# Spare PSUM banks behind each group of eight, later bounds for the weight splits of the attention loop, and fixed places of the y and m tiles

## The chip, the cores and the metric

The kernel runs on one core of a Trainium2 chip. The metric is the device time of one execution in microseconds (us); of several runs the median is given, with the lowest and the highest. All clock statements are about the clock granted to TensorE in the profile: 1.00 is 2.4 GHz and 0.50 is 1.2 GHz.

## The reference

Two transformer blocks run one after the other on 256 tokens of 1024 channels, in fp32. Cut to what carries the work:

```python
# block 1
h = rms_norm(x, pre_mix_norm)
mix = hybrid_mixer(h, w_in, ...)          # RG-LRU, gated linear attention, block attention
x = x + rms_norm(mix @ w_out, post_mix_norm)
h = rms_norm(x, pre_ffn_norm)
x = x + rms_norm((silu(h @ w_gate) * (h @ w_up)) @ w_down, post_ffn_norm)   # d_ff = 2816

# block 2, layers l = 0 and 1
sh1, sc1, g1, sh2, sc2, g2 = split(silu(c) @ w_ada[l] + b_ada[l], 6)
h = x * (1 + sc1) + sh1
if l == 0:
    b, cc, v = split(h @ conv_w_in, 3)
    y = (b * causal_conv3(cc * v)) @ conv_w_out
else:
    k, v, logf = shared_kv(x, c, ...)      # once
    y = forgetting_attention(h, w_q, k, v, logf, w_o)   # 16 heads, softmax(q k / 8 + F[t] - F[s]) v
x = layer_norm(alpha * x + g1 * y, ...)
h = x * (1 + sc2) + sh2
y = (silu(h @ w_gate[l]) * (h @ w_up[l])) @ w_down[l]   # d_ff = 2816
x = layer_norm(alpha * x + g2 * y, ...)
```

The three feed-forward parts are called ffn0 (block 1), ffn1 and ffn2 (block 2) below; the mixer of layer 0 is "the convolution", that of layer 1 "the attention loop".

## The kernel before

**Products.** Activations are kept transposed: a matrix of 256 tokens x 1024 channels is eight tiles of 128 channels x 256 tokens (`NK` = 8; the inner width of a feed-forward part is 22 tiles, `NFF` = 22). Each fp32 product is done in three TensorE matmuls on a split of both factors into a rounded high and a low remainder: high weights by high activation, low weights by high activation, high weights by low activation. `mm3` (L159) issues them for one weight block of 128x128 (L162, L163, L164). The activation is the moving operand, 256 columns wide.

The moving tiles have names by their role: `xh`/`xl` the input of a product, `yh`/`yl` a second set of eight (the mixer's output, or the input of a feed-forward part, by turns), `mh`/`ml` the inner activations of a feed-forward part. `hl_tiles` (L256) makes x and y tiles of T + 2 = 258 columns, of which 256 are used; the evacuation in `ffn` makes m tiles of the same size. Tiles stand in SBUF one after the other, 1056 bytes apart; the pool of the x and y tiles is `xp`, that of the m tiles the pool of each feed-forward part (`fp`).

**Weights.** There are 2336 weight blocks, in the order of use. `weights` (L130) loads them eight at a time into a raw tile (four buffers, one DMA each on SP's queue, L127), rounds them into `wh` on ScalarE (L144) and subtracts on VectorE for `wl` (L150); `wh` and `wl` have five buffers each, 4096 bytes apart in a partition.

**Vectors of the modulation.** The products with `w_ada` are matrix by vector; `gemv` (L360) does them on VectorE in 112 passes `gw` (L371), each with a load of its own on SP's queue (L368, three buffers).

**Groups.** Where the input comes tile by tile, `kouter` (L223) goes over the input tiles outside and eight output columns inside (`ksteps` L190: L197 high by high, L198 low weights, L203 or L200 low activation): eight columns of 256 fill four PSUM banks. These are all four buffers of the pool `pacc`. Every feed-forward part has such a group near its start (after a few columns done by `lazy`, L1041), the convolution one at its start. After the group the other columns of a feed-forward part come in pairs (`pair` L176: gate and up of one inner tile, 48 matmuls into one bank of `pacc`), those of the convolution as singles (`single` L168, 24 matmuls). PSUM has two more pools: `plg` with two banks (tag `lg`, the attention's logits) and `pms` with two.

**Evacuation.** `evac` in `ffn` (L906) takes gate and up out of PSUM: in ffn0 both are first multiplied by a row (L909, L911, `ff_g`, `ff_u`), then silu on ScalarE (L522), the product `ff_m` on VectorE (L914 or L918), `mh` on ScalarE (L921), `ml` on VectorE (L922). In the convolution loop (L1207 to L1224) `c_c` (L1212) and `c_up` (L1215) read PSUM.

**Attention loop** (L1304 to L1320). Each of its eight iterations i makes the next query tile (`wq`), the logits of two heads (`fox_logits` L766), the transposes of the last softmax (`fox_pt` L800, matmuls at L805), its product with the values (`fox_pv` L813), a step of the output projection, and the softmax (`fox_softmax` L784: row maxima L793, exponentials L794 on ScalarE, reciprocal L795, four scalings of `a_L` L797 on VectorE). TensorE's order is that of the code there.

**Order on the other engines.** The framework places instructions by a simulated timeline; what is fixed by hand is an order without a wait: `after(i, a)` (L383) puts i behind a on the same engine. `weights` puts each split behind an entry of the list `self.bound` once `self.free` splits have gone; `gemv` puts a pass behind `self.gbound` and behind the last split. `unbroken` (L377) sets these: ahead of the attention loop to the last gemv bound, and after its first iteration to the last row maximum of that softmax (`self.mxs`):

```python
    def unbroken(self, ins, free, act=None, head=None):
        self.bound, self.free, self.abound, self.first = ins, free, act, head
        self.gbound = ins[-1]
```

Of the kernel before, what the change touches and what calls it, by code (L numbers as in the profile page):

```python
# [9 lines left out]
F32 = mybir.dt.float32  # L10
# [4 lines left out]
ALU = mybir.AluOpType  # L15
# [20 lines left out]
EARLY = 4  # L36
EXP_LN = 6
WARM = (3, 3, 5, 0)
G_ROWS = 80
# [25 lines left out]
class Net:  # L65
# [101 lines left out]

    def single(self, wname, c, X, nk=NK, fill=True):  # L168
        t = self.acc([P, T])
        for k in range(nk):  # L170
            self.mm3(t, wname, k, c, X[0][k], X[1][k], k == 0, k == nk - 1)
        if fill:
            self.fill(nk / NK)
        return t

    def pair(self, w0, c0, w1, c1, X):  # L176
        t = self.acc([P, 2, T])
        for j, (w, c) in enumerate(((w0, c0), (w1, c1))):
            for k in range(NK):
                self.mm3(t[:, j, :], w, k, c, X[0][k], X[1][k], k == 0 and j == 0, k == NK - 1 and j == 1)  # L180
        self.fill(2)
        return t
# [49 lines left out]
    def tokmajor(self, wname, c0, nt, X):  # L232
# [21 lines left out]
        return outs  # L254

    def hl_tiles(self, tag, pool=None):  # L256

        w = T + 2
        h = self.tl(pool or self.xp, [P, w], tag + "h", F32R, NK)
        l = self.tl(pool or self.xp, [P, w], tag + "l", F32R, NK)  # L260
        return h, l, h[:, 0:T], l[:, 0:T]
# [522 lines left out]
    def fox_softmax(self, lg):  # L784

        V, A = self.nc.vector, self.nc.scalar
        mx = self.tmp("a_mx", (P, 4))
        sm = self.tmp("a_sm", (P, 4))
        Ls = [self.tmp("a_L", (P, 384), bufs=4) for _ in range(2)]
        part = [(hh, j, s) for hh in range(2) for j, s in ((0, slice(0, T)), (1, slice(T, 384)))]  # L790
        for hh, j, s in part:
            c = slice(2 * hh + j, 2 * hh + j + 1)
            self.mxs = V.tensor_reduce(mx[:, c], lg[hh][:, s], AX.X, ALU.max, negate=True)  # L793
            self.fn = A.activation(Ls[hh][:, s], lg[hh][:, s], AF.Exp, bias=mx[:, c], accum_out=sm[:, c])  # L794
        V.reciprocal(sm, sm)  # L795
        for hh, j, s in part:
            V.tensor_scalar(Ls[hh][:, s], Ls[hh][:, s], sm[:, 2 * hh + j:2 * hh + j + 1], None, ALU.mult)  # L797
        return Ls
# [101 lines left out]
    def ffn(self, l, X, R=None, first=(), rows=None):  # L900

        nc = self.nc
        V = nc.vector
        MH, ML = [], []

        def evac(g, u):  # L906
# [8 lines left out]
            else:  # L915
                s = self.silu(g)
                m = self.tmp("ff_m")
                V.tensor_tensor(m, s, u, ALU.mult)  # L918
            h = self.tl(self.fp, [P, T + 2], "mh", F32R)[:, 0:T]
            lo = self.tl(self.fp, [P, T + 2], "ml", F32R)[:, 0:T]  # L920
            nc.scalar.activation(h, m, AF.Copy)  # L921
            V.tensor_tensor(lo, m, h.bitcast(F32), ALU.subtract)  # L922
            MH.append(h)
# [11 lines left out]
        for j in range(n + 4, NFF):  # L935
            ps = self.pair(wg, j, wu, j, X)
            self.drain()
            evac(ps[:, 0, :], ps[:, 1, :])
# [140 lines left out]
    def run(self):  # L1079
# [10 lines left out]
        for k in range(NK):  # L1090
            h, l = self.hilo(self.x0[k], "x", self.vec("pre_mix_norm", k))
            X[0].append(h)
            X[1].append(l)
        for k in range(NK):
            sq = self.tmp("p_sq")
# [111 lines left out]
        for i in range(NK):  # L1207
            for w in ("ci_c", "ci_v", "ci_b"):
                if (w, i) not in got:
                    got[(w, i)] = self.single(w, i, X)  # L1210
            c = self.tmp("c_c")
# [91 lines left out]

        self.unbroken([self.gbound], 2)  # L1304
        with self.tc.manual_schedule(engines={nc.tensor.engine}):
# [3 lines left out]
            for i in range(NK + 1):  # L1309
# [7 lines left out]
                Ls = self.fox_softmax(lg) if i < NK else None  # L1317
                if i == 0:
                    self.unbroken([self.gbound, self.mxs], 0)
                q = qn  # L1320
# [164 lines left out]
```

## Time and profile before

| what | us |
|---|---|
| median of 3 runs (lowest to highest) | 987.88 (987.56 to 987.98) |
| the profiled execution, its own time | 985.9 |
| its span, first to last instruction | 984.2 |
| TensorE busy with matmuls | 927.9 (94%), 7434 matmuls |
| VectorE busy | 768.8 (78%) |
| ScalarE busy | 530.2 (54%) |
| GpSimd busy | 19.7 (2%) |
| DMA | 219.56 MB, 223 GB/s over the span |

The profile is one execution, taken by the hardware profiler. PE is TensorE (PEld its weight loads), DVE is VectorE, ACT is ScalarE, POOL is GpSimd and SP is SyncE. Times are in microseconds; a group of instructions is named by its line of the kernel, its engine, its operation and its tiles as output<-inputs. Matmuls are pipelined: one record is longer than its distance to the next, so that a pace is read from the records' number in a stretch. An entry in square brackets at the end of a timeline's row is the idle time ahead of that instruction and what ended it; "x8" merges eight instructions in a row.

### The profile page before, as it was taken

Reading aid. Unit: us, or ns where it says so; the run is one execution under the profiler, and the core shown is the slowest. Engines: PE = TensorE matmul, PEld = TensorE weight load, DVE = VectorE, ACT = ScalarE, POOL = GpSimd, SP = SyncE. Lnnn points to the kernel's source line nnn. Section 1 sums busy time; section 2 is a strip of 40 time slices with the busy share of each in tenths; the row PEclk is TensorE's granted clock in tenths of the full one; section 3 lists DMA queues with packets and bytes.
Section 4 is the critical chain, followed back from the end, with each engine's and each line's share of the span. In section 5 each row is a group of like instructions: output and inputs, shape, how many; then the busy total and the mean of one; then the engine's idle time right before and its main releaser. Section 6 shows DMA issues by size and latency. Waiting matters only on the chain.

```text
span 984.2 us, 19003 instructions
## 1 busy us (share of the span) xinstructions
PE 927.9 (94%) x7434; PEld 893.6 (91%) x7434; DVE 768.8 (78%) x1471; ACT 530.2 (54%) x951; POOL 19.7 (2%) x66
## 2 busy tenths in 40 slices
PE   7989997999999999998899999999699999999996
PEld 7879896999999899998899999987587899999995
DVE  7896678999988588679899899796764897665553
ACT  7484653554444555548555454377365586554331
POOL 1111000000000000000000000000000000000001
PEclk9999998999999999999999999999799999999998
DMA  8754337899999477544999999454642257655531
GB/s 291 249 197 129 108 108 278 294 330 327 318 336 390 142 255 250 179 134 155 320 341 356 329 368 348 167 176 145 250 150 65 87 153 275 214 184 183 191 108 43
DMA packets 62346, 219.56 MB, mean 223 GB/s; under 512 B 7112, under 2 KB 8784, under 8 KB 62256
## 3 DMA queue, kind: packets, MB, share of 16 engines
q1 hardware_dynamic: 61056, 215.06, 63.7%
q0 software_dynamic: 1056, 3.16, 1.0%
q8 instruction: 58, 0.95, 0.4%
q14 instruction: 32, 0.26, 0.1%
q10 hardware_dynamic: 144, 0.13, 0.0%
HBM read 217.26 MB, written 2.63 MB: 223 GB/s over the span
## 4 chain that ended last, share of the span: by engine, by line
PE 80%; DVE 12%; ACT 4%; issue 3%; DMA 2%; DVEq 0%; ACTq 0%
PE acc L162 20%; PE acc L164 20%; PE acc L163 20%; PE acc L197 4%; DVE wl L150 4%; PE acc L198 4%; PE acc L203 3%; DMA raw<-wts 1%; ACT wh L144 1%; DVE gw L371 1%; PE acc L251 1%; PE acc L253 1%; PE acc L252 1%; PE ms L820 1%; PE lg L773 1%
## 5 line engine op out<-in xcount | busy, mean ns | idle before, releaser
L150 DVE TENSOR_TENSOR wl<-raw,wh 128x1024 fp32r<-128x1024 f32 (+2 forms) x296 | 356.2, 1209 | 102.4 <-ACT wh L144 101.0
L144 ACT ACTIVATE wh<-raw 128x1024 fp32r<-128x1024 f32 (+2 forms) x296 | 307.6, 1046 | 225.4 <-PE acc L164 128.2
L162 PE MATMUL acc<-yh,wh 128*128 128x256 f32 x608 | 171.1, 282 | 7.0 <-DVE ff_m L918 5.6
L162 PE MATMUL acc<-xh,wh 128*128 128x256 f32 x576 | 164.2, 285 | 8.9 <-DVE ff_u L911 7.2
L164 PE MATMUL acc<-yl,wh 128*128 128x256 f32 x608 | 171.3, 282 | 0.0
L163 PE MATMUL acc<-yh,wl 128*128 128x256 f32 x608 | 170.6, 281 | 0.0
L163 PE MATMUL acc<-xh,wl 128*128 128x256 f32 x576 | 162.9, 283 | 1.4 <-DVE wl L150 1.4
L164 PE MATMUL acc<-xl,wh 128*128 128x256 f32 x576 | 163.0, 283 | 0.0
L163 PE MATMUL acc<-mh,wl 128*128 128x256 f32 x528 | 148.1, 281 | 0.0
L164 PE MATMUL acc<-ml,wh 128*128 128x256 f32 x528 | 148.1, 281 | 0.0
L162 PE MATMUL acc<-mh,wh 128*128 128x256 f32 x528 | 147.9, 281 | 0.0
L371 DVE SCALAR_TENSOR_TENSOR gw<-gw,cact 128x1024 f32<-128x1024 f32 x112 | 134.7, 1221 | 0.6 <-DMA gw<-ada 0.4
L162 PEld LDWEIGHTS acc<-yh,wh 128*128 128x128 f32 x608 | 115.2, 190 | 7.6 <-DVE ff_m L918 6.1
L162 PEld LDWEIGHTS acc<-xh,wh 128*128 128x128 f32 x576 | 109.9, 191 | 11.3 <-DVE ff_u L911 7.4
L163 PEld LDWEIGHTS acc<-yh,wl 128*128 128x128 f32 x608 | 115.2, 190 | 0.4 <-issue 0.4
L164 PEld LDWEIGHTS acc<-yl,wh 128*128 128x128 f32 x608 | 114.9, 189 | 0.6 <-issue 0.6
L163 PEld LDWEIGHTS acc<-xh,wl 128*128 128x128 f32 x576 | 110.1, 191 | 1.8 <-DVE wl L150 1.6
L164 PEld LDWEIGHTS acc<-xl,wh 128*128 128x128 f32 x576 | 109.8, 191 | 0.1
L162 PEld LDWEIGHTS acc<-mh,wh 128*128 128x128 f32 x528 | 99.5, 189 | 0.0
L164 PEld LDWEIGHTS acc<-ml,wh 128*128 128x128 f32 x528 | 99.4, 189 | 0.0
L163 PEld LDWEIGHTS acc<-mh,wl 128*128 128x128 f32 x528 | 99.3, 188 | 0.0
L197 PE MATMUL acc<-xh,wh 128*128 128x256 f32 (+1 forms) x256 | 67.7, 294 | 8.7 <-ACT wh L144 5.5
(399 smaller groups left out, 1493.2 us busy)
## 6 DMA issues: line engine op xcount, KB each, us to landing
raw<-wts SPq DMA_DIRECT2D x288, 512.0 KB, 4.5
gw<-ada SPq DMA_DIRECT2D x112, 512.0 KB, 5.6
raw<-wts SPq DMA_DIRECT2D x6, 256.0 KB, 5.9
m_scr<-m_row POOLq DMA_DIRECT2D x2, 768.0 KB, 5.8
ax<-xT SPq DMA_DIRECT2D x4, 256.0 KB, 4.8
m_b<-m_scr POOLq DMA_DIRECT2D x8, 128.0 KB, 3.6
out<-fg SPq DMA_DIRECT2D x8, 128.0 KB, 1.8
cst<-cst SPq DMA_DIRECT2D x1, 588.5 KB, 7.1
```

The source lines that it names most:

```text
L144: i = self.aw = nc.scalar.activation(self.wh[:, d], r, AF.Copy)
L150: self.anchor = nc.vector.tensor_tensor(self.wl[:, d], r, self.wh[:, d].bitcast(F32), ALU.subtract)
L162: m = [mm(ps, wh, xh, start=start, stop=False), mm(ps, wl, xh, start=False, stop=False), mm(ps, wh, xl, start=False, stop=stop)]
L163: mm(ps, wl, xh, start=False, stop=False),
L164: mm(ps, wh, xl, start=False, stop=stop)]
L197: m.append(mm(outs[i], wh, X[0][k], start=k == 0 and i % per == 0, stop=False))
L198: m.append(mm(outs[i], wl, X[0][k], start=False, stop=False))
L203: m.append(mm(outs[i], wh, X[1][k], start=False, stop=False))
L251: mm(outs[tt], h, wh, start=k == 0 and (tt == 0 or not one), stop=False)
L252: mm(outs[tt], l, wh, start=False, stop=False)
L253: mm(outs[tt], h, wl, start=False, stop=k == NK - 1 and (tt == 1 or not one))
L371: i = nc.vector.scalar_tensor_tensor(t, t, 1.0, self.cact, op0=ALU.mult, op1=ALU.mult, accum_out=self.ada[:, g:g + 1])
```

## The change

- `pair` and `single` get an argument `spare`: their output then stands in a bank of the pool `plg` (tag `lg`) in place of `pacc`. It is set for the first two pairs behind the k-outer group of each feed-forward part, and for the first two singles behind that of the convolution.
- `shift` makes a tile that nobody reads, with a memset on GpSimd: 96 bytes in `xp` ahead of the y tiles, and 160 bytes in the pool of each feed-forward part ahead of the m tiles. y and m tiles are made 256 columns wide in place of 258, so that they stand 1024 bytes apart; the x tiles stay. With that every y tile starts 96 bytes, and every m tile 320 bytes, behind the place of the weight tiles modulo 512.
- The evacuation of a feed-forward part sets `self.gbound` to its last subtraction (`ml`): a gemv pass emitted later comes behind it.
- In the attention loop the bounds are renewed after each softmax: splits emitted from then on come behind the last scaling of the softmax before (`self.alast`, handed on in `al`), gemv passes behind the last scaling of this one.

```diff
--- before.py
+++ after.py
@@ -35,6 +35,7 @@
 POUT = (0, 1)
 EARLY = 4
 EXP_LN = 6
+SHIFT = (96, 160)
 WARM = (3, 3, 5, 0)
 G_ROWS = 80
 RSQ_SEED = 1595953144
@@ -165,16 +166,16 @@
         if self.strict:
             self.chain(m)
 
-    def single(self, wname, c, X, nk=NK, fill=True):
-        t = self.acc([P, T])
+    def single(self, wname, c, X, nk=NK, fill=True, spare=False):
+        t = self.tl(self.plg, [P, T], "lg") if spare else self.acc([P, T])
         for k in range(nk):
             self.mm3(t, wname, k, c, X[0][k], X[1][k], k == 0, k == nk - 1)
         if fill:
             self.fill(nk / NK)
         return t
 
-    def pair(self, w0, c0, w1, c1, X):
-        t = self.acc([P, 2, T])
+    def pair(self, w0, c0, w1, c1, X, spare=False):
+        t = self.tl(self.plg, [P, 2, T], "lg") if spare else self.acc([P, 2, T])
         for j, (w, c) in enumerate(((w0, c0), (w1, c1))):
             for k in range(NK):
                 self.mm3(t[:, j, :], w, k, c, X[0][k], X[1][k], k == 0 and j == 0, k == NK - 1 and j == 1)
@@ -253,9 +254,13 @@
                 mm(outs[tt], h, wl, start=False, stop=k == NK - 1 and (tt == 1 or not one))
         return outs
 
+    def shift(self, pool, n):
+
+        self.nc.gpsimd.memset(self.tl(pool, [P, n // 4], "pad", bufs=1), 0.0)
+
     def hl_tiles(self, tag, pool=None):
 
-        w = T + 2
+        w = T + 2 if tag == "x" else T
         h = self.tl(pool or self.xp, [P, w], tag + "h", F32R, NK)
         l = self.tl(pool or self.xp, [P, w], tag + "l", F32R, NK)
         return h, l, h[:, 0:T], l[:, 0:T]
@@ -794,7 +799,7 @@
             self.fn = A.activation(Ls[hh][:, s], lg[hh][:, s], AF.Exp, bias=mx[:, c], accum_out=sm[:, c])
         V.reciprocal(sm, sm)
         for hh, j, s in part:
-            V.tensor_scalar(Ls[hh][:, s], Ls[hh][:, s], sm[:, 2 * hh + j:2 * hh + j + 1], None, ALU.mult)
+            self.alast = V.tensor_scalar(Ls[hh][:, s], Ls[hh][:, s], sm[:, 2 * hh + j:2 * hh + j + 1], None, ALU.mult)
         return Ls
 
     def fox_pt(self, Ls):
@@ -902,6 +907,7 @@
         nc = self.nc
         V = nc.vector
         MH, ML = [], []
+        self.shift(self.fp, SHIFT[1])
 
         def evac(g, u):
             if R is not None:
@@ -916,10 +922,10 @@
                 s = self.silu(g)
                 m = self.tmp("ff_m")
                 V.tensor_tensor(m, s, u, ALU.mult)
-            h = self.tl(self.fp, [P, T + 2], "mh", F32R)[:, 0:T]
-            lo = self.tl(self.fp, [P, T + 2], "ml", F32R)[:, 0:T]
+            h = self.tl(self.fp, [P, T], "mh", F32R)
+            lo = self.tl(self.fp, [P, T], "ml", F32R)
             nc.scalar.activation(h, m, AF.Copy)
-            V.tensor_tensor(lo, m, h.bitcast(F32), ALU.subtract)
+            self.gbound = V.tensor_tensor(lo, m, h.bitcast(F32), ALU.subtract)
             MH.append(h)
             ML.append(lo)
 
@@ -933,7 +939,7 @@
         for ps in self.kouter([(w, n + j) for j in range(4) for w in (wg, wu)], X, False):
             evac(ps[:, 0, :], ps[:, 1, :])
         for j in range(n + 4, NFF):
-            ps = self.pair(wg, j, wu, j, X)
+            ps = self.pair(wg, j, wu, j, X, j < n + 6)
             self.drain()
             evac(ps[:, 0, :], ps[:, 1, :])
         return MH, ML
@@ -1091,6 +1097,7 @@
             h, l = self.hilo(self.x0[k], "x", self.vec("pre_mix_norm", k))
             X[0].append(h)
             X[1].append(l)
+        self.shift(self.xp, SHIFT[0])
         for k in range(NK):
             sq = self.tmp("p_sq")
             i = A.activation(sq, self.x0[k], AF.Square)
@@ -1207,7 +1214,7 @@
         for i in range(NK):
             for w in ("ci_c", "ci_v", "ci_b"):
                 if (w, i) not in got:
-                    got[(w, i)] = self.single(w, i, X)
+                    got[(w, i)] = self.single(w, i, X, spare=(w, i) in order[8:10])
             c = self.tmp("c_c")
             A.activation(c, got[("ci_c", i)], AF.Copy)
             up = self.tmp("c_up", (P, T + 2))
@@ -1301,7 +1308,8 @@
             for j, t in enumerate(self.fox_pv(i, pts, vs)):
                 Y[j].append(t)
 
-        self.unbroken([self.gbound], 2)
+        al = self.gbound
+        self.unbroken([al], 2)
         with self.tc.manual_schedule(engines={nc.tensor.engine}):
             q = wq(0)
             Ls = None
@@ -1315,8 +1323,8 @@
                 if i:
                     out(i - 1, pts)
                 Ls = self.fox_softmax(lg) if i < NK else None
-                if i == 0:
-                    self.unbroken([self.gbound, self.mxs], 0)
+                if i < NK:
+                    self.bound, self.gbound, al = [al], self.alast, self.alast
                 q = qn
                 self.drain()
             step(Y, NK - 1)
```

## Rows read from the trace of the kernel before

**Rows 1.** The page: busy time and instructions of each engine; the chain by engine
```profile
PE 927.9 (94%) x7434; PEld 893.6 (91%) x7434; DVE 768.8 (78%) x1471; ACT 530.2 (54%) x951; POOL 19.7 (2%) x66
...
PE 80%; DVE 12%; ACT 4%; issue 3%; DMA 2%; DVEq 0%; ACTq 0%
```

**Rows 2.** TensorE's waits: who waited for whom, us in total, times, longest
```profile
PE ms L805 <- DVE a_L L797: 9.8, 2, 9.5
PE acc L162 <- DVE ff_u L911: 7.2, 1, 7.2
PE acc L162 <- DVE ff_m L918: 5.6, 2, 3.7
...
PE acc L198 <- DVE wl L150: 2.0, 3, 0.9
...
PE acc L162 <- DVE c_up L1215: 1.1, 1, 1.1
```

**Rows 3.** Windows: us; busy (instructions) by engine; granted clock, DMA share, GB/s
```profile
157.30:164.40 7.10, 0.00 (x0) 0.00 (x0) 7.10 (x12) 1.74 (x3) 0.00 (x0) 0.83 0.84 269
164.40:168.70 4.30, 4.24 (x20) 4.24 (x21) 4.30 (x12) 2.02 (x6) 0.00 (x0) 0.50 1.01 406
...
478.40:482.90 4.50, 4.43 (x24) 4.43 (x25) 4.35 (x11) 2.02 (x6) 0.00 (x0) 0.62 1.03 409
692.40:701.60 9.20, 0.00 (x0) 0.00 (x0) 9.20 (x17) 4.00 (x8) 0.00 (x0) 0.62 0.93 349
705.90:708.50 2.60, 2.60 (x15) 2.60 (x15) 0.42 (x1) 0.15 (x1) 0.00 (x0) 0.56 0.10 38
```

**Rows 4.** Timeline (start, us, what), first block, after its k-outer group
```profile
155.67 2.36 DVE L150 TENSOR_TENSOR wl<-raw,wh 128x1024 fp32r<-128x1024 f32 x2
...
159.09 2.36 DVE L150 TENSOR_TENSOR wl<-raw,wh 128x1024 fp32r<-128x1024 f32 x2
...
164.46 0.58 PE L162 MATMUL acc<-xh,wh 128*128 128x256 f32 x1 [7.24 <-DVE ff_u L911]
```

**Rows 5.** Timeline of the first softmax in the attention loop
```profile
689.22 0.37 ACT L794 ACTIVATE a_L<-lg,a_mx 128x128 f32<-128x128 f32 x1
...
695.93 0.18 DVE L795 RECIPROCAL a_sm<-a_sm 128x4 f32<-128x4 f32 x1
...
701.22 1.01 DVE L797 TENSOR_SCALAR a_L<-a_L,a_sm 128x256 f32<-128x256 f32 x4
...
701.83 0.48 PE L805 MATMUL ms<-ident,a_L 128*128 128x128 f32 x1 [9.50 <-DVE a_L L797]
```

**Rows 6.** Timeline of k-outer groups, first and second block: one moving tile repeated
```profile
152.42 1.10 PE L203 MATMUL acc<-xl,wh 128*128 128x256 f32 x8
...
466.23 0.63 PE L197 MATMUL acc<-yh,wh 128*128 128x256 f32 x4
...
468.13 1.12 PE L203 MATMUL acc<-yl,wh 128*128 128x256 f32 x8
...
470.91 1.07 PE L203 MATMUL acc<-yl,wh 128*128 128x256 f32 x8
```

**Rows 7.** Windows of TensorE alone: us, busy (matmuls), clock, DMA share, GB/s
```profile
838.00:888.00 50.00, 50.00 (x428) 1.00 0.62 197
905.00:955.00 50.00, 50.00 (x425) 1.00 0.51 167
```

**Rows 8.** Groups of instructions of the page: y and m as moving tiles
```profile
L162 PE MATMUL acc<-yh,wh 128*128 128x256 f32 x608 | 171.1, 282 | 7.0 <-DVE ff_m L918 5.6
...
L162 PE MATMUL acc<-mh,wh 128*128 128x256 f32 x528 | 147.9, 281 | 0.0
```

**Rows 9.** Timeline of a later iteration of the attention loop
```profile
714.47 0.39 PE L162 MATMUL acc<-xh,wh 128*128 128x256 f32 x1
...
716.26 1.01 DVE L797 TENSOR_SCALAR a_L<-a_L,a_sm 128x256 f32<-128x256 f32 x4
...
717.29 1.23 DVE L150 TENSOR_TENSOR wl<-raw,wh 128x1024 fp32r<-128x1024 f32 x1
```

## The prediction

> **What bounds the kernel now.** I read the page's busy shares and its chain first: TensorE is busy 94% of the span and is 80% of the chain that ended last [rows 1]. So time goes in two ways only: TensorE standing still, or its matmuls following each other more slowly than they could. The second view is the list of TensorE's waits [rows 2]. Its four large entries name one event each or a pair: 9.8 us for softmax results in the attention loop (a_L, L797), 7.2 us and 5.6 us for the evacuations that follow the k-outer groups of the feed-forward blocks (ff_u L911, ff_m L918), 1.1 us for the same in the convolution (c_up L1215). Third, the windows over those places [rows 3]: TensorE issues nothing, VectorE is busy all the time, and in three of four places the granted clock stands at 0.50 to 0.62 afterwards (1.2 GHz for most of it) though the matmuls are back to back. Last, the pace of dense stretches, which the page can't show: 428 matmuls in 50 us with y as moving operand, 425 with m [rows 7]. A matmul record is 0.28 us long, so that is 50.28/428 = 117.5 ns and 50.28/425 = 118.3 ns each.
>
> **Spare banks.** A k-outer group fills all four acc banks at its end, so the next pair must wait until bank 0 is read. Was it the bank alone? The timeline of the first block says so [rows 4]: the split weights (wl) of that pair's two tiles are finished by 158.03, those of the next two by 161.45, while the pair starts at 164.46, released by ff_u. Two pairs are 96 matmuls, 11.3 us at 117.5 ns; bank 0 is free long before that, so the third pair won't wait. I cost the removed waits at their whole length: 7.2 + 5.6 us. In the convolution the two singles cover 5.6 us; its 1.1 us go (and a wait under half a microsecond behind it, which I leave out). The slow clock after the stalls goes with them. After the first block 20 matmuls took 4.30 us in place of 20 x 0.1175 = 2.35, so 1.95; after the second 24 took 4.50 in place of 2.82, so 1.7 [rows 3]. After the third block's wait (5.6 less its longest, 3.7, is 1.9) I know of no slow stretch. Sum: 13.9 us of waits + 3.65 us of clock = 17.5 us.
>
> What hid under those waits? VectorE's work: 7.10 us of 7.10 busy [rows 3]. It isn't removed, it must now run beside matmuls. Cover: each later weight tile is read 24 matmuls (2.82 us) after the one before it, and the two tiles finished at 161.45 would be read from 162.8 and 165.6, so some 4 us of lead remain there, and the gemv passes (gw, 1.22 us each) are what can move back. That is what the new bound on gemv passes (behind the last evacuation's lo) does: in the first block it also takes passes from in front of the evacuations. The price if that cover isn't enough is bounded by 0 and by what the stall gave back, 7.2 + 1.95 = 9.1 us. I take 2 us, as the nearest row in kind is TensorE's waiting for a wl, 2.0 us in three pieces [rows 2]. Passed queues: the gw loads on SP's queue wait for a gemv's buffer, and raw weight loads stand behind them; with three gw buffers and four raw tiles I cost this at nothing, and within the same 9.1 us if the cover fails.
>
> **Attention loop.** The exponentials of the first softmax are done at 689.6, yet the reciprocal runs at 695.93 and the four scalings end at 702.2 [rows 5]. Between them VectorE runs gemv passes and weight splits of later iterations without a break [rows 3]; they may, since their bound is only the last row maximum of this softmax. TensorE stands for 9.5 us until the scalings release it at 701.83. After the change a split emitted in iteration i waits for the softmax of i-2, a gemv pass for that of i-1. So reciprocal and scalings (0.18 + 1.01 us) follow the exponentials: 689.7 + 1.2 = 690.9, before TensorE wants them. The whole 9.8 us goes, and with it the slow clock: 15 matmuls took 2.60 us, at 117.5 ns 1.76, so 0.8 [rows 3]. Next late is the copy of the transposes (a_pt) or a split: bounds 0 and one gemv pass or split, 1.22 us, per step; I take 1 us for the first iterations. Queued behind a waiting split on VectorE are the row maxima of the next softmax; they need logits that TensorE makes after that split's weights are needed, so in order nothing new waits. Sum: -9.8 - 0.8 + 1.0 = -9.6 us.
>
> **Places of the moving tiles.** All weight tiles start at one place modulo 512 (4096 bytes apart). x, y and m tiles now lie 1056 bytes apart, so successive ones start at all multiples of 32 modulo 512; in the order of use the h tiles of a k-outer group lie 0, 224, 192, 160, 128, 96, 64, 32 bytes behind the weights, the l tiles 256 more. In such a group one tile streams 8 to 16 times in a row, so the trace of before holds constant places already. Eight L203 matmuls in a row take seven paces and one record: at 468.13 (sixth k step, place 352) 1.12 us, (1.12-0.28)/7 = 120 ns; at 470.91 (seventh, place 320) 1.07, so 113 ns; at 152.42, the same place 320 in the first block, 1.10, so 117 ns [rows 6]. Engine, shape and clock are the same in all three. So the place matters, and at 320 two paces are possible. The new place of y is 96: there the 16 matmuls on the h tile of the sixth step run from 466.23 to 468.13, 119 ns with the change of tile, and pass into the 120 ns of its l tile, so I take 120 ns for y. For m at 320 I take the middle of 113 and 117.1, 115.1 ns, since the rows show both.
>
> The Trainium skill speaks against this part: "SBUF — State Buffer", section "Who interferes with whom", holds that PE never waits on another reader, and "TensorE: Matmul & The Clock Gate", section "Step-by-step: what each phase is for", that loading the next weights takes no read bandwidth from the running matmul. By these the places change nothing. The 113 and 120 ns above disagree.
>
> Counts: y 3 x 608 in pairs and singles [rows 8], and 26 columns x 8 x 3 = 624 in the k-outer groups and the two partial products: 2448 x (120 - 117.5) = +6.1 us. m 3 x 528 [rows 8]: 1584 x (115.1 - 118.3) = -5.1 us, with ends -8.4 (all at 113) and -1.9 (all at 117.1). If y could be had at 113 it would be -11.0. The two pads cost one POOL memset each on an engine that is 2% busy: nothing, as nobody reads them.
>
> **Sum.** The profiled execution took 985.9 us, 1.7 more than its span; the median of the runs shown is 987.88, 2.0 above it. 985.9 - 17.5 + 2.0 - 9.6 + 6.1 - 5.1 = 961.8 in the profiled execution's terms; 963.8 as a median.
>
> **Rivals.**
> (a) y doesn't behave in pairs as in the groups (there h, h, l alternate, here one tile repeats) and runs as fast as the settled 113 to 115 ns: 2448 x 5 to 7 ns = 12 to 17 us less, 947 to 952. For: at 320 one place has two paces. Against: at 96 and 352 the rows show 119 and 120 only. Chance 0.18.
> (b) The places change nothing, the rule above: without +6.1 - 5.1, 962.8. Chance 0.07, inside the forecast's own spread (957 to 970, from m's ends and waits between 0 and 5 us).
> (c) The stalls are half given back: VectorE was busy for all of them, the splits fall behind in the first block (9.1 us back) or the attention stall moves to the next split (up to 5 us back). 973 to 978. Chance 0.15.
> (d) Slower than before: in the attention loop the splits come to stand behind the softmax of the same iteration. In a later iteration the scalings end at 717.27, the split at 718.5, while the weight matmuls start at 714.47 [rows 9]: a wait of 4.0 us in each of the six iterations that split weights, 24 us, and up to 1.7 us of slow clock after each, as after the second block's stall [rows 3], together 24 to 34 us: 963.8 + 24 to 34 = 988 to 998, about 993. It decides from 24 us, 4 us an iteration. Against: by the code a split waits only for the softmax two iterations back, so it would have to run a whole iteration late. Chance 0.04.
> The forecast itself has 0.56. That the change doesn't do what it says is in (c) and (d).
>
> Faster by over 0.2% (about what a measurement of this kernel can tell from no change): 0.95; within: 0.01; slower: 0.04. The range takes (a) in its upper end and (c) in its lower one: 949 to 976.
>
> **What would show it.** TensorE's list of waits without L805, ff_u and ff_m over 1 us; no stretch at half clock after the three blocks' k-outer groups or at 706; a waiting L163 or L198 for wl in the first block would show (c). In the windows of 50 us, y at 419 matmuls (120 ns) and m at 430 to 445; y above 430 is rival (a), 428 and 425 unchanged rival (b). The scalings of the first softmax within 2 us of its exponentials; a wl right behind a_L with TensorE's L162 waiting for it in each iteration is (d). I am wrong outright if the sum of TensorE's idle time doesn't fall by 20 us or more.

## The result and the profile after

The changed kernel took 959.07 us (median of 3 runs, 957.72 to 960.63) against 987.88: a ratio of 0.971, interval 0.9686 to 0.9734. Six more runs beside other kernels gave 960.99 us and 0.9732 (0.9707 to 0.9757). The forecast was 963.8. The profiled execution took 959.07 us with a span of 957.4, 26.8 us shorter than before. All lines of the kernel behind the edits move down by one to eight; L162 to L164 are now L163 to L165, L797 is L802, L805 is L810.

The page, busy times and the chain by engine, which answer to [rows 1]:

```profile
PE 923.0 (96%) x7434; PEld 890.4 (93%) x7434; DVE 767.0 (80%) x1471; ACT 527.1 (55%) x951; POOL 20.2 (2%) x70
...
PE 85%; DVE 9%; ACT 2%; DMA 2%; issue 2%; DVEq 0%; SPq 0%; ACTq 0%
```

TensorE has the same 7434 matmuls, and its share of the chain has grown from 80% to 85%, VectorE's has fallen from 12% to 9%. TensorE's waits (who waited for whom, us in total, times, longest), against [rows 2]:

```profile
PE acc L198 <- ACT wh L145: 5.5, 1, 5.5
...
PE acc L199 <- DVE wl L151: 1.9, 3, 0.9
PE acc L198 <- ACT xh L271: 1.8, 1, 1.8
...
PE ms L313 <- DVE nw_y L294: 1.5, 2, 1.3
...
PE ms L810 <- ACT a_pt L814: 0.6, 1, 0.6
```

The entries for ff_u and ff_m at L163 and for c_up are gone, that for a_L is down to 0.3 us. What leads the list now (wh, 5.5 us) stood in the kernel before too. The waits for wl (L199) are 1.9 us, as before 2.0: nothing was given back there. Two waits have grown, those for xh (L198) and nw_y (L313). They belong to the norm at the end of the first block; before they were

```profile
PE acc L197 <- ACT xh L266: 0.7, 1, 0.7
PE ms L308 <- DVE nw_y L289: 0.7, 3, 0.3
```

The windows over the places of [rows 3] (us, length, then busy time and number of instructions of PE, PEld, DVE, ACT, POOL, granted clock, DMA share, GB/s): behind the first two groups of eight of the feed-forward parts, then the first softmax of the attention loop:

```profile
156.80:163.90 7.10, 7.10 (x63) 7.10 (x62) 6.98 (x11) 2.33 (x5) 0.00 (x0) 1.00 0.79 233
461.00:468.00 7.00, 7.00 (x61) 7.00 (x60) 5.83 (x8) 5.98 (x11) 0.00 (x0) 1.00 0.85 290
672.00:680.00 8.00, 7.75 (x71) 6.68 (x69) 4.62 (x11) 4.42 (x13) 0.00 (x0) 1.00 0.11 44
```

Behind both groups TensorE is busy without a gap, at clock 1.00, while VectorE works 6.98 of 7.10 us in the first: the stall is covered, not its work removed. In the attention loop TensorE is busy for 7.75 of 8 us. The timeline of the first softmax shows why, against [rows 5]:

```profile
676.29 0.37 ACT L799 ACTIVATE a_L<-lg,a_mx 128x128 f32<-128x128 f32 x1
...
676.78 0.18 DVE L800 RECIPROCAL a_sm<-a_sm 128x4 f32<-128x4 f32 x1 [0.53 <-ACT a_L L799]
...
676.99 1.01 DVE L802 TENSOR_SCALAR a_L<-a_L,a_sm 128x256 f32<-128x256 f32 x4
...
678.43 0.28 PE L786 MATMUL lg<-cmask,identb 128*128 128x256 bf16 x1
...
678.55 0.27 PE L810 MATMUL ms<-ident,a_L 128*128 128x128 f32 x1
```

The exponentials end at 676.66, reciprocal and scalings follow within 1.4 us, before it took 12.6; the transposes (L810) start right behind the last mask matmul (L786). Last the dense stretches, against [rows 7], y and then m:

```profile
800.00:850.00 50.00, 50.00 (x419) 1.00 0.72 220
885.00:935.00 50.00, 50.00 (x427) 1.00 0.45 143
```

y runs at 50.28/419 = 120.0 ns, m at 50.28/427 = 117.8 ns; before it was 117.5 and 118.3.

### The profile page after: what moved, and what is told of

Its sections match the earlier page's. It is cut to its first block, busy times and chain, and to the rows that moved or that the text cites. A ratio compares the mean times of both kernels' runs of the same rounds, so it can differ in the third digit from the quotient of the medians.

```text
span 957.4 us, 18988 instructions
## 1 busy us (share of the span) xinstructions
PE 923.0 (96%) x7434; PEld 890.4 (93%) x7434; DVE 767.0 (80%) x1471; ACT 527.1 (55%) x951; POOL 20.2 (2%) x70
## 4 chain that ended last, share of the span: by engine, by line
PE 85%; DVE 9%; ACT 2%; DMA 2%; issue 2%; DVEq 0%; SPq 0%; ACTq 0%
PE acc L163 19%; PE acc L164 19%; PE acc L165 19%; PE acc L198 5%; PE acc L199 5%; PE acc L204 4%; DVE wl L151 3%; PE lg L163 1%; PE lg L165 1%; PE lg L164 1%; PE acc L254 1%; PE acc L252 1%; PE acc L253 1%; DMA raw<-wts 1%; PE acc L201 1%
## 5 line engine op out<-in xcount | busy, mean ns | idle before, releaser
L163 PE MATMUL acc<-yh,wh 128*128 128x256 f32 x544 | 153.7, 283 | 0.9 <-ACT yh L271 0.9
L164 PE MATMUL acc<-yh,wl 128*128 128x256 f32 x544 | 153.3, 282 | 0.0
L165 PE MATMUL acc<-yl,wh 128*128 128x256 f32 x544 | 152.6, 281 | 0.5 <-DVE yl L272 0.5
L163 PE MATMUL acc<-xh,wh 128*128 128x256 f32 x528 | 148.8, 282 | 0.5 <-ACT g_v L659 0.5
L165 PE MATMUL acc<-xl,wh 128*128 128x256 f32 x528 | 148.3, 281 | 0.0
L164 PE MATMUL acc<-xh,wl 128*128 128x256 f32 x528 | 147.9, 280 | 0.0
L164 PE MATMUL acc<-mh,wl 128*128 128x256 f32 x528 | 147.4, 280 | 0.0
L163 PE MATMUL acc<-mh,wh 128*128 128x256 f32 x528 | 147.4, 279 | 0.0
L165 PE MATMUL acc<-ml,wh 128*128 128x256 f32 x528 | 147.0, 279 | 0.0
L165 PEld LDWEIGHTS acc<-yl,wh 128*128 128x128 f32 x544 | 103.0, 190 | 0.8 <-DVE yl L272 0.7
L163 PEld LDWEIGHTS acc<-yh,wh 128*128 128x128 f32 x544 | 101.8, 187 | 1.1 <-ACT yh L271 1.1
L164 PEld LDWEIGHTS acc<-yh,wl 128*128 128x128 f32 x544 | 102.2, 188 | 0.0
L163 PEld LDWEIGHTS acc<-xh,wh 128*128 128x128 f32 x528 | 99.4, 188 | 2.2 <-ACT g_v L659 1.0
L164 PEld LDWEIGHTS acc<-xh,wl 128*128 128x128 f32 x528 | 99.5, 188 | 0.2
L165 PEld LDWEIGHTS acc<-xl,wh 128*128 128x128 f32 x528 | 99.3, 188 | 0.1
L163 PEld LDWEIGHTS acc<-mh,wh 128*128 128x128 f32 x528 | 99.2, 188 | 0.0
L164 PEld LDWEIGHTS acc<-mh,wl 128*128 128x128 f32 x528 | 98.9, 188 | 0.0
L165 PEld LDWEIGHTS acc<-ml,wh 128*128 128x128 f32 x528 | 98.8, 187 | 0.0
L198 PE MATMUL acc<-xh,wh 128*128 128x256 f32 (+1 forms) x256 | 66.8, 292 | 9.6 <-ACT wh L145 5.5
```

The source lines that it names most:

```text
L163: m = [mm(ps, wh, xh, start=start, stop=False), mm(ps, wl, xh, start=False, stop=False), mm(ps, wh, xl, start=False, stop=stop)]
L164: mm(ps, wl, xh, start=False, stop=False),
L165: mm(ps, wh, xl, start=False, stop=stop)]
L198: m.append(mm(outs[i], wh, X[0][k], start=k == 0 and i % per == 0, stop=False))
```

## Experiments

Kernels timed together on one chip share the runs of the kernel before; its median was 986.18, 985.78, 986.85 and 987.75 us in the four groups, so ratios are compared where kernels of different groups meet. Paces without a fence are means over all matmuls of a kernel's trace that have y or m as moving tile and follow one another at full clock (some 2400 and 1580). Where the text gives the time of a stretch by matmuls, it is counted in the profiled execution, from the start of one numbered matmul of the 7434 to that of another. The code cuts show the lines that matter, not whole edits.

**The parts alone.** `places_alone` takes the kernel before and adds only the places (`shift` and `SHIFT = (96, 160)` are as in the change):

```diff
-        w = T + 2
+        w = T + 2 if tag == "x" else T
+        self.shift(self.xp, SHIFT[0])       # 96 bytes ahead of the y tiles
+        self.shift(self.fp, SHIFT[1])       # 160 bytes ahead of the m tiles
-            h = self.tl(self.fp, [P, T + 2], "mh", F32R)[:, 0:T]
+            h = self.tl(self.fp, [P, T], "mh", F32R)        # ml alike
```

> The kernel before with the places alone: y tiles 96 bytes, m tiles 320 bytes behind the weights' place modulo 512, no spare bank, no new bound. Theory (pace depends on the place): y slows from 117.5 to 119.9 ns on 2448 matmuls, +5.7 us, m gains 0.8 ns on 1584, -1.3 us: 987.9 + 4.4 = 992.3 us, slower. Rival as predicted blind (+6.1 - 5.1): 988.9. Rival that places change nothing and y's slower pace in the changed kernel comes from VectorE running closer behind: 987.9, and y at 117.5 ns in the dense stretches.

Measured: 988.16 us in 10 runs, ratio 1.0019 (1.0001 to 1.0038), so +1.9 us (0.1 to 3.7) where 4.4 was expected; by the time alone the 1.0 of the prediction isn't told apart from it, the paces decide. y is at 120.0 ns, as expected. m isn't at one pace. Windows of TensorE in two of the three m stretches:

```profile
570.00:610.00 40.00, 40.00 (x342) 1.00 0.97 355
912.00:952.00 40.00, 40.00 (x355) 1.00 0.61 193
```

The second feed-forward part's m runs at 40.28/342 = 117.8 ns, the third's at 40.28/355 = 113.5, same place, same code, same clock. So m at 320 has two paces, and which one a stretch falls into isn't set by the program's text. A stretch of 528 matmuls is worth 528 x 4.3 ns = 2.3 us, which is nearly all of the missing 2.5 us, if the profiled execution stands for the others.

**The spare banks with their bound.** `spare_alone` is the changed kernel without the edit of the attention loop (cut below) and without the places, so it holds the spare banks and the gemv bound behind the evacuations:

```diff
-                if i < NK:
-                    self.bound, self.gbound, al = [al], self.alast, self.alast
+                if i == 0:
+                    self.unbroken([self.gbound, self.mxs], 0)
```

> The kernel before with the spare banks and the gemv bound behind each evacuation, without the new bounds in the attention loop and without the places. Theory: the stalls behind the groups of eight go whole with their slow clock, 987.9 - 17.5 = 970.4 us, TensorE's waits for ff_u, ff_m and c_up gone, the 9.8 us wait for a_L unchanged. Rival of the prediction (2 us given back in waits for wl): 972.4. Rival that half is given back: 976 to 980.

Measured: 968.22 us, ratio 0.9816 (0.9797 to 0.9836), -18.0 us where the sum has -17.5. The largest wait left to TensorE is the one the part doesn't touch, here 10.2 us:

```profile
PE ms L810 <- DVE a_L L802: 10.2, 2, 10.0
```

So the stalls behind the groups are gone whole, with their slow clock. But something came back, at another place. The norm at the end of the first block, in the changed kernel:

```profile
326.91 1.22 DVE L376 SCALAR_TENSOR_TENSOR gw<-gw,cact 128x1024 f32<-128x1024 f32 x1
...
328.05 0.42 DVE L1199 TENSOR_TENSOR ax<-ax,fg 128x256 f32<-128x256 f32 x1
...
329.67 0.39 PE L198 MATMUL acc<-xh,wh 128*128 128x256 f32 x1 [1.83 <-ACT xh L271]
```

Three gemv passes (at 324.15, 326.91 and 328.72) now lie between the norm's short steps on VectorE, where before there was none, and TensorE waits for nw_y and xh. From the 2400th to the 2550th matmul it took 21.1 us before, 23.2 in the changed kernel, 23.3 in `spare_alone` and 21.1 in `no_evac_bound` below: the bound behind the evacuations costs 2.2 us there. That the sum still came out at -18.0 is in part luck: 2.8 us of the gain lie in the attention loop, where two short stretches at half clock are gone, and the first 1050 matmuls took 3.8 us longer in this profiled execution than in that of the kernel before, which isn't traced to any part.

`attn_alone` is the kernel before with the edit of the attention loop alone:

```diff
-                    self.unbroken([self.gbound, self.mxs], 0)
+                    self.bound, self.gbound, al = [al], self.alast, self.alast
...
-            V.tensor_scalar(Ls[hh][:, s], ...)
+            self.alast = V.tensor_scalar(Ls[hh][:, s], ...)
```

> The kernel before with the new bounds of the attention loop alone (no spare banks, no bound behind the evacuations, places as before). Theory: the 9.8 us wait for a_L goes with 0.8 us of slow clock and nothing comes back, 987.9 - 10.6 = 977.3 us. The prediction's step (1 us back in the first iterations): 978.3. Rival that the stall moves to a later split or gemv pass: 982 to 988. The ff_u and ff_m waits stay at 7.2 and 5.6 us.

Measured: 982.52 us in 10 runs, ratio 0.9967 (0.995 to 0.9984): -3.3 us, and the rival's 982 to 988 holds. The a_L wait is gone but for 0.3 us, but TensorE now waits for a_pt (1.58 and 2.9 us at L825). The timeline around the first of them, of several engines (SPq is SP's queue of DMA issues; a merged row starts with its first instruction):

```profile
686.18 1.22 DVE L376 SCALAR_TENSOR_TENSOR gw<-gw,cact 128x1024 f32<-128x1024 f32 x1
...
686.29 1.47 SPq L373 DMA_DIRECT2D gw<-ada  x2
...
687.33 1.22 DVE L151 TENSOR_TENSOR wl<-raw,wh 128x1024 fp32r<-128x1024 f32 x1
...
688.62 6.05 SPq L128 DMA_DIRECT2D raw<-wts  x3
...
693.22 1.06 ACT L145 ACTIVATE wh<-raw 128x1024 fp32r<-128x1024 f32 x1 [2.46 <-DMA raw<-wts]
...
695.11 0.48 ACT L814 ACTIVATE a_pt<-ms 128x384 f32<-128x384 f32 x1
...
695.65 0.65 PE L825 MATMUL ms<-a_pt,ax 128*64 128x256 f32 x2 [1.58 <-ACT a_pt L814]
```

Two gemv passes (685.03 and 686.18) stand on VectorE ahead of the split wl, which ends at 688.55 and frees its raw tile; the next raw load goes at 688.62. The split wh on ScalarE waits 2.46 us for that load, a_pt stands behind wh (with a copy and an exponential between them), and L825 behind a_pt. The obvious suspect, the two gw loads that stand ahead of the raw load on SP's queue, isn't what holds it: both are issued by 687.8. Around the loop every raw load in the traces of before, after, `attn_alone` and `no_evac_bound` goes within 0.1 us of the end of the split four tiles earlier, whose buffer it takes (one, in `no_evac_bound`, within 0.4). In the changed kernel the same passes lie in front of the loop:

```profile
666.65 1.22 DVE L376 SCALAR_TENSOR_TENSOR gw<-gw,cact 128x1024 f32<-128x1024 f32 x1
...
666.76 1.47 SPq L373 DMA_DIRECT2D gw<-ada  x2
...
667.79 1.22 DVE L151 TENSOR_TENSOR wl<-raw,wh 128x1024 fp32r<-128x1024 f32 x1
...
669.04 0.33 SPq L128 DMA_DIRECT2D raw<-wts  x1
...
673.96 1.06 ACT L145 ACTIVATE wh<-raw 128x1024 fp32r<-128x1024 f32 x1 [1.38 <-DMA raw<-wts]
...
679.07 0.87 ACT L814 ACTIVATE a_pt<-ms 128x384 f32<-128x384 f32 x2 [1.77 <-PE ms L812]
...
679.61 1.25 PE L825 MATMUL ms<-a_pt,ax 128*64 128x256 f32 x8 [0.25 <-ACT a_pt L814]
```

There the same split ends at 669.01, the raw load goes at 669.04, and the copies of a_pt follow the transposes. The edit of the loop alone moves the scalings but leaves these passes, and with them the raw tile, late. Beside the spare banks and the evacuations' bound the same edit is worth more: `no_places`, below, is `spare_alone` with it, and their ratios, 0.9816 and 0.9679 (0.9656 to 0.9701), differ by 0.0137, 13.5 us with some 3 us of uncertainty. The loop itself, from the 5250th to the 5850th matmul, took 92.5 us before, 86.7 in `attn_alone`, 89.7 in `spare_alone`, 79.3 in `no_places` and 79.9 in the changed kernel. So in the loop the edit is worth 5.8 us alone and 10.4 beside the other two parts; the rest of the 13.5 is within that uncertainty.

**The bound behind the evacuations.** `no_evac_bound` is the changed kernel without it:

```diff
-            self.gbound = V.tensor_tensor(lo, m, h.bitcast(F32), ALU.subtract)
+            V.tensor_tensor(lo, m, h.bitcast(F32), ALU.subtract)
```

> The changed kernel without the gemv bound behind each evacuation's last subtraction. If that bound is what keeps the splits ahead in the first feed-forward part, TensorE waits there for wl or for an evacuation again: 2 to 9 us, 961 to 968 us. Rival that the gemv passes find room in any order: 959 us, no wait over 1 us behind the group of eight.

Measured: 977.17 us, ratio 0.9903 (0.9868 to 0.9938). Against the changed kernel's 0.971 and 0.9732 that is 0.017 to 0.019, 17 to 19 us more, twice the upper end of what was expected. TensorE's waits show two places:

```profile
PE acc L163 <- DVE ff_u L917: 6.3, 1, 6.3
PE ms L825 <- ACT a_pt L814: 5.8, 4, 2.9
```

The first is in the first feed-forward part, some 35 us behind the group of eight (columns as above):

```profile
195.58 1.22 DVE L376 SCALAR_TENSOR_TENSOR gw<-gw,cact 128x1024 f32<-128x1024 f32 x1
...
196.72 1.22 DVE L376 SCALAR_TENSOR_TENSOR gw<-gw,cact 128x1024 f32<-128x1024 f32 x1
...
198.20 1.22 DVE L151 TENSOR_TENSOR wl<-raw,wh 128x1024 fp32r<-128x1024 f32 x1
...
199.34 0.41 DVE L917 TENSOR_TENSOR ff_u<-acc,R 128x256 f32<-128x256 f32 x1
...
199.90 0.55 PE L163 MATMUL acc<-xh,wh 128*128 128x256 f32 x1 [6.28 <-DVE ff_u L917]
```

Gemv passes and a split stand on VectorE ahead of the evacuation, the pair waits 6.28 us for ff_u, and 23 matmuls after it run at half clock (2.2 us more than at full clock). Right behind the group nothing waits without the bound either: the 150 matmuls across it (1050th to 1200th) took 27.0 us before and 17.6 here as in the changed kernel. So the spare bank alone takes that stall away, and the bound keeps it from coming back further on. The second place is the a_pt wait in the attention loop, again behind gemv passes: they start at 680.14 and 681.29, the split behind them ends at 683.66, the raw load goes at 683.72, and wh waits 2.60 us for its tile until 688.46; the loop took 89.2 us. So this one bound works in both places. That it settles the loop's order through where the gemv passes come to lie is read from these traces; how the framework's order comes about wasn't tried apart.

**Is it the place, and relative to what?** `y_unplaced` and `y_320` change the pads of the changed kernel:

```diff
-        w = T + 2 if tag == "x" else T
+        w = T + 2
-        self.shift(self.xp, SHIFT[0])
-SHIFT = (96, 160)
+SHIFT = (96, 256)      # y_unplaced, with the two edits above; m stays at 320
+SHIFT = (320, 448)     # y_320, without them; m stays at 320
```

> The changed kernel with the y tiles as before (258 columns, 1056 bytes apart, no pad ahead of them), m tiles still at 320. Theory: y goes back to 117.5 ns, 2448 x 2.4 ns = 5.7 us less than the changed kernel's 959.1: 953.4 us. Rival that y's pace is not a matter of its place: 959.1, y stays at 119.9 ns. m stays at 117.8 ns by both.

Measured: 955.39 us, ratio 0.9692 (0.9668 to 0.9715); y back at 117.7 ns, m at 117.8.

> The changed kernel with y at 320 in place of 96, m at 320 as it was. Theory that the place alone sets the pace: y takes m's 117.8 ns, 2448 x 2.1 = 5.2 us less, 953.9 us. Second: at 320 two paces are possible, and y falls into the faster, 113.3 ns: 959.1 - 2448 x 6.6 ns = 943 us. Third, any common place of all tiles is slower than changing ones: y stays near 120 ns, 959 us.

Measured: 956.72 us, ratio 0.9699 (0.9679 to 0.9719); y at 117.7 ns. The paces came as the first theory has them in both; the times went its way by 1 to 4 us, with intervals that overlap that of the changed kernel.

`place_scan` leaves out the rest of the kernel and runs threes of matmuls alone:

```python
for i in range(n):                       # n = 8; wo, o, ol in columns of 4 bytes
    b = wo + 128 * (i % 8)
    mm(ps, wh[:, b:b + P], h[:, o:o + T], ...)
    mm(ps, wl[:, b:b + P], h[:, o:o + T], ...)
    mm(ps, wh[:, b:b + P], l[:, ol:ol + T], ...)
```

> Only matmuls, nothing of the reference is computed: no other engine works and no DMA moves while TensorE runs. Threes as in the kernel (high weights by h, low weights by h, high weights by l), eight weight blocks in turn, h and l at one place p behind the weights modulo 512, p from 0 to 496 in steps of 16 bytes, four stretches of 24 matmuls for each p, each begun by a matmul of another width so that they start at other phases; then four places with the weights 64 bytes further, and three with l 128 bytes behind h. Theory (pace follows the distance between the moving tile and the weights, with two possible paces at some): near 120 ns at 96 and 352, 117.8 or 113.3 at 64, 192, 320 and 448, the same for p and p + 256; with the weights moved by 64, what was at 0 appears at 64. Rival (the moving tile's own place counts): the weights' shift changes nothing. Rival (VectorE's, ScalarE's and the DMAs' traffic sets the pace): one pace at all places, under 117 ns.

The profile's timeline, TensorE, the second and last high-by-h matmul of a stretch at 96, then of two stretches at 192 (each pair is 18 matmuls apart):

```profile
98.59 0.28 PE L37 MATMUL ps<-h,wh 128*128 128x256 f32 x1
...
100.75 0.28 PE L37 MATMUL ps<-h,wh 128*128 128x256 f32 x1
```

```profile
169.50 0.28 PE L37 MATMUL ps<-h,wh 128*128 128x256 f32 x1
...
171.62 0.28 PE L37 MATMUL ps<-h,wh 128*128 128x256 f32 x1
...
172.44 0.28 PE L37 MATMUL ps<-h,wh 128*128 128x256 f32 x1
...
174.48 0.28 PE L37 MATMUL ps<-h,wh 128*128 128x256 f32 x1
```

At 96 it is (100.75 - 98.59)/18 = 120.0 ns; at 192 (171.62 - 169.50)/18 = 117.8 and (174.48 - 172.44)/18 = 113.3, from two starts. The mean paces of the four stretches of each place (ns, worked out from the starts in the same way, the first six of 24 left out):

```
place p (and p + 256)   four starts
  0    119.6 to 119.7        128   118.4 to 120.0
 16    113.4 to 118.7        144   116.6 to 119.0
 32    116.5 to 116.9        160   117.4 to 118.6
 48    118.4                 176   119.2 to 119.4
 64    117.7 to 117.8        192   113.3 to 117.8
 80    118.5 to 120.2        208   119.1 to 119.2
 96    119.8 to 120.2        224   118.2 to 118.6
112    114.8 to 115.8        240   116.9 to 117.4
weights 64 bytes further, distances 0, 32, 96, 448: 119.7 to 120.0, 116.7 to 117.9, 119.7 to 119.8, 113.3 to 117.8
(place 256 gave up to 120.0)
```

While they ran no other engine worked and no load or store of the program moved, so traffic is not the cause. The weights' shift moved the pattern with it: the distance counts, modulo 256. With l 128 bytes behind h, at places 0, 64 and 96 of h, the paces were 116.5 to 118.1, 117.8 to 117.9 and 118.1 to 118.7.

> Only matmuls again, nothing of the reference is computed. Places p in steps of 4 bytes from 0 to 252 without the multiples of 16 (h and l alike, three stretches of 30 each), then all pairs of different places of h and l in steps of 32 (two stretches each). In steps of 16 the paces lay between 113.3 and 120.2 ns, with 114.8 to 115.8 at 112 in all four stretches. If pace is a smooth matter of the place, the neighbours of 112 (104 to 120) stay under 116 ns and those of 96 near 120; if only the 16-byte grain counts, 4, 8 and 12 beside a place repeat it. Pairs of different places lie between their two paces if each matmul pays for its own place, outside of them if the order counts; the changing places of the kernel before took 117.5.

Of the 48 places on the 4-byte grain, 28 and 236 were the best from all starts (115.5 to 115.6), 104 the worst (129.7 from two starts, 120.1 from the third). Neither guess held: 108 and 116, beside the good 112, gave 120.0 and 121.5 to 121.8, and 16 is not repeated by 12 or 20. The 56 pairs of different places of h and l gave 116.5 to 121.3, many of them 117.5 to 118.5, like the changing places of the kernel before. Some lie outside of the paces of their two places (h at 0 with l at 128: 116.5 and 117.7), so the combination counts too.

**No places, and better ones.** Beside the changed kernel, on the same chip: `no_places` undoes the place edits shown under `places_alone`; `p32` has `SHIFT = (32, 448)`; `p112` has

```diff
-            self.wh = self.tl(self.whp, [P, CB * P], "wh", F32R)
+            self.wh = self.tl(self.whp, [P, CB * P + P], "wh", F32R)[:, 4:4 + CB * P]    # wl alike
-SHIFT = (96, 160)
+SHIFT = (128, 448)
```

> The changed kernel once more, beside the next three on the same chip: 0.971 of the kernel before, 957 to 959 us; y at 119.9 ns, m at 117.8 ns unless one of its three stretches falls into 113.3 (2.4 us less for each).

> The changed kernel without the places: spare banks and both bounds stay, y and m tiles as before. Theory: y gains 2.3 ns on 2448 matmuls, m loses 0.8 on 1584: 5.7 - 1.3 = 4.4 us less than the changed kernel on this chip. Rival that the places cost nothing here (the three-round comparison of the places alone gave +2.0 us with 4 us of uncertainty): the same time.

> The changed kernel with y and m 32 bytes behind the weights (pads 32 and 448 in place of 96 and 160). By the scan 116.5 to 116.8 ns there from all starts: y 3.3 x 2448 = 8.1 us, m 1.2 x 1584 = 1.9 us, 10 us less than the changed kernel. Rival as for 112.

> The changed kernel with y and m 112 bytes behind the weights (the weight tiles moved by 16 bytes, pads 128 and 448). By the scan, 114.8 to 115.8 ns there from all four starts: y 119.9 to 115.3 on 2448 matmuls, m 117.8 to 115.3 on 1584: 11.3 + 4.0 = 15 us less than the changed kernel. x, now at odd multiples of 16, is not known: 116 to 119 ns, up to 4 us either way. Rival that a map taken without the other engines' work does not hold in the kernel: y and m at 117 to 120.

| kernel | median, us (lowest to highest) | ratio to before | y, ns | m, ns |
|---|---|---|---|---|
| changed | 960.99 (958.76 to 963.1) | 0.9732 (0.9707 to 0.9757) | 119.9 | 117.8 |
| no_places | 956.18 (954.58 to 957.16) | 0.9679 (0.9656 to 0.9701) | 117.6 | 118.6 |
| p32 | 953.77 (950.61 to 954.83) | 0.9649 (0.9621 to 0.9677) | 117.2 | 117.1 |
| p112 | 956.7 (952.25 to 966.46) | 0.9698 (0.9651 to 0.9746) | 117.8 | 117.3 |

Without the places the kernel is 4.8 us faster, where 4.4 was expected. Its two dense stretches are back at the numbers of before:

```profile
800.00:850.00 50.00, 50.00 (x428) 1.00 0.72 224
885.00:935.00 50.00, 50.00 (x425) 1.00 0.42 127
```

`p32` is the fastest, 7.2 us under the changed kernel, less than the 10 expected. It has two paces as well:

```profile
510.00:560.00 50.00, 50.00 (x427) 1.00 0.94 344
885.00:935.00 50.00, 50.00 (x431) 1.00 0.40 119
```

50.28/427 = 117.8 ns in the second feed-forward part (here y and some m), 50.28/431 = 116.7 in the third. `p112` missed its 15 us: 4.3 us less by the medians, and its runs spread over 14 us. In its profile y and m run at 116.7, 118.3 and 119.8 ns by stretch, never at the 115 of the scan. Why a long stretch in the kernel doesn't settle where 24 matmuls alone did stays open.

## Why the prediction was right

A gain of 2.4% was forecast and 2.9% came; the time lies in the likeliest case's own spread. Below, the traces of before and after are taken apart: the time from one matmul's start to the next counts as a wait when it is over 0.26 us, else as pace at full or at half clock, each against a mean of 118.2 ns. By the steps of the prediction:

- **Stalls, -17.5.** Right. The waits are gone, with the clock at 1.00 behind the groups: -15.4 of waits and -3.3 of slow clock, -18.7 in all. That the bank alone held the pair is shown by `no_evac_bound`.
- **New waits in the first block, +2.0.** Right in size, +2.2, but at another place: not for wl behind the group but in the norm at the end of the block, for nw_y and xh. The cover behind the group held because of the bound on gemv passes, and that bound is what puts passes into the norm. Its price if it is gone, up to 9.1 us in the prediction, measured 6.3 us of wait and 2.2 us of slow clock there, as sized.
- **Attention loop, -9.6.** Under-sized: -10.0 of waits and -3.1 of slow clock, -13.1 in all. The scalings follow the exponentials in 1.4 us, and the later waits (a_pt 0.6 and 0.3, a_L 0.3 us) come to about the 1.0 taken. The term for the clock, 0.8, took one of three stretches at half clock in the loop; two more stood there and are gone, and one is new (rows below). `spare_alone` hasn't got the two either, so this gain doesn't hang on the loop's edit alone. The step "passed queues, at nothing" stands: no trace shows SP's queue holding a raw load back by over 0.4 us around the loop. What it missed is the raw tile's buffer, which VectorE frees late when gemv passes stand ahead of the split. Of the edit's 10.4 us in the loop 5.8 are left when it stands alone, and the prediction tied the bound that prevents this to the first block.
- **y, +6.1.** 419 matmuls in 50 us, as written; over the trace 117.6 became 119.95 ns, +2.35 x 2448 = +5.8. This step costs time, and without the places the kernel is faster.
- **m, -5.1.** Mis-sized: 118.6 to 117.8, -0.8 x 1584 = -1.3 us, outside the ends -8.4 and -1.9. The middle of two paces was taken; a stretch takes one of them, and in this profile all three took the slower, 117.8. One in three took 113.5 in `places_alone`. The upper end should have been that slower pace in the form the kernel uses, with changes between h and l, not in the groups' repeats.
- **From profile to median, +2.0.** Not there: the profiled execution was the median run.

The stretches at half clock in the loop that the prediction left out, two of the kernel before and one of the kernel after (TensorE alone: us, busy and number, clock, DMA share, GB/s):

```profile
756.00:759.40 3.40, 3.40 (x16) 0.50 0.51 154
776.40:779.90 3.50, 3.50 (x16) 0.51 0.22 77
```

```profile
732.30:735.70 3.40, 3.40 (x19) 0.50 0.17 63
```

Put in again: -18.7 + 2.2 - 13.1 + 4.1 (the pace of all matmuls at full clock, where y and m by themselves give +4.5) = -25.5 of the span's -26.8; the rest are small waits that no step names. The forecast missed by 4.7 us, up to rounding: the loop 3.5, the stalls 1.2, the small waits 1.4 and 2.0 between profile and median, less 3.1 for the places, which cost 4.1 in place of 1.0, and less 0.2 for the new waits. Errors of both signs cancelled in part, so the time came nearer than the worst of its terms.

Rival (a) fell: y above 430 matmuls didn't come. Rival (b), that places change nothing, falls by `place_scan`: 113.3 to 120.2 ns with nothing else running. Its time, 962.8, lay so near the forecast that the total couldn't tell it; the pace did. (The rule of the Trainium skill that stood behind it, "SBUF — State Buffer", section "Who interferes with whom", is that TensorE never waits on another reader. These runs had no other reader and so don't test it; what was drawn from it, that places change nothing, fails, since the pace went with the distance of TensorE's own two operands. By what path no run shows.) Rival (c) didn't come in this kernel beyond the 2.2 us above, but `no_evac_bound` is (c) in both its places. Rival (d) fell: no wl stands behind a softmax with TensorE waiting.

## What to carry to other kernels

A stall behind a group that fills all banks goes whole when the next products have another bank, if the work under the stall is ordered so that nothing else becomes late; take the order and the bank as one edit. Work that is pushed back comes to lie somewhere: look for a short chain, such as a norm, that it now stands in. When an edit moves work on one engine, look at each buffer which that engine frees: a load that takes it starts later, and so does every engine that waits for the load. Before a queue is blamed, compare the time of the issue with the end of the instruction that freed the buffer. Cost an address change from the pace of the same sequence of operands, over several stretches, and judge it apart from the edits beside it: here a part that cost 5 us was hidden in a gain of 29.

## What the hardware showed

A 256-column matmul in a dense stretch at full clock took 113.3 to 129.7 ns by the distance of its moving tile from its weights, modulo 256 bytes, with no other engine at work. At some distances the same sequence holds either of two paces: at 192 in the scan 113.3 or 117.8 ns, by how it starts; at 320 in the kernel 113.5 or 117.8, and what chooses there stays open, since in the scan 64 and 320 gave 117.7 to 117.8 from every start. The changing distances of the kernel before came to 117.6 ns for y and 118.6 for m.
